# A streaming encoder on one core: rows turned in blocks for three pairs, and projections of whole width

## The chip, the cores and the metric

The kernel runs on one core of a Trainium2 chip. The metric is the device time of one execution in microseconds. Five engines work on it, each with an instruction stream of its own that runs in order: TensorE (PE; its weight loads are listed apart as PEld), VectorE (DVE), ScalarE (ACT), GpSimd (POOL) and SyncE (SP), which here only issues transfers. Transfers run on 16 DMA engines.

## The reference

One layer of a streaming encoder with 2048 new frames of one stream ("prompt") and 64 of a running one ("sample"), width 1024. Cut to what matters:

```python
aq, ak, av, ag, hq, hf, hi, hg = jnp.split(rms_norm(x, ln_g) @ w_in, SPLITS, axis=-1)
k, v = heads(ak), heads(av)                      # 8 heads of 64
o_a = attn_fn(heads(aq), k, v) * silu(ag)        # chunks of 64 frames, 576 keys, learned bias
o_b, S = hgrn2_branch(hq, hf, hi, hg, lb, norm_g, s0)   # 4 heads of 128, gated recurrence
y = x + concat([o_a, o_b]) @ w_out
...
y_prompt = rms_norm(hp, ln_f_g)
new_k_prompt, new_v_prompt                       # the last 512 frames' K and V rows
```

The outputs that the change touches are the last 512 rows of K and V, one row per frame, and the last rows of `y_prompt`.

## The kernel before

**Tiling.** The frames are taken in four super-blocks of 512, 576 (with the sample's 64), 512 and 512 frames (`SUPER`). In each, 32 projections follow (`JOBS`): for each of four groups hf, hq, hi, hg (one recurrence head) and pg, pq, pk, pv (gate, Q, K and V of a pair of attention heads). In the last super-block the last twelve come in another order, and end with pk and pg of the last pair. One projection gives 128 features by the frames of the block: `project` does 24 matmuls, since x and the weights are split into a high and a low part (w_hi x_hi, w_hi x_lo, w_lo x_hi, eight pieces each). Normally it runs over all 512 frames at once (128x512). The first two projections of a super-block run in halves of 256 frames, interleaved (first half of one, first half of the other, then the second halves), since the second half's x (tiles xh and xl) is filled later; the last two run in halves too, which lets the next block's x replace the first half early.

**Behind a projection** stands its evacuation, which takes the accumulator "acc" out of PSUM. Features lie on the partitions, so K and Q are used as they come. V must have frames on the partitions. There are two ways for that. `ev_v` (super-blocks 1 to 3) transposes 32x32 blocks on DVE straight from the accumulator into a tile "vT" (`turn_blocks`), moves the blocks into place through a scratch in DRAM (`turn_rows`: four transfers out, "way<-vT", and one back, "vT<-way"), and splits the result into high and low parts (`split_rows`: a cast on ACT, a subtraction on DVE). `ev_v_last` (last super-block) copies to "vT", transposes on PE (`tr<-ident,vT`), and splits from PSUM. The K and V rows of the last super-block go out by `new_rows`: four transposes on PE, a copy to a tile "sig", one transfer of 256 KB.

**Order.** The program is written out by a planner (`Plan`) before it is compiled: each stage is a Python thread that yields until its data, its engine's queue or a token is there; `project` emits two matmuls and lets the others go on. The planner's own times decide the order on each engine and are not run times. Tokens stand for buffers: "sig" two, "vT" three, "acc" two, weights "w" four, "ck" one. The gates (`silu_to`: three ACT steps into a "sig" tile and a DVE product into "sga") use "sig" too.

**The end.** When the last projection is done, `out_load` reads the mixed heads back ("sig<-mixd", "vT<-mixd"), and the output product follows: 56 steps of 12 matmuls of 128x512 with weights that come from scratch (`wo_load`, "w<-wod"), beside the last attention. `out_norm` ends each tile of 128 frames: a square on ACT for each half of 512 columns, 1/sqrt on ACT, the product with r and the gain on DVE, and a transfer.

Of the kernel before, what the change touches and what calls it, by code (L numbers as in the profile page):

```python
# [8 lines left out]
F32 = mybir.dt.float32  # L9
# [3 lines left out]
ALU = mybir.AluOpType  # L13
# [4 lines left out]
P = 128  # L18
D = 1024
# [4 lines left out]
NPAIR = 4  # L24
# [22 lines left out]
JOBS = [[(k, g) for g in range(4) for k in ("hf", "hq", "hi", "hg", "pg", "pq", "pk", "pv")] for _ in SUPER]  # L47
# [136 lines left out]
def hymba_step(  # L184
# [439 lines left out]
    def new_rows(src, off, bn, p, out_p, out_s, tok, t):  # L624

        full = bn // P
        segs = [(a, b, rows, out) for a, b, rows, out in ((0, full, P, out_p), (full, full + 1, bn - full * P, out_s))
                if rows and out is not None]
        if not segs:
            tok.put(1, t)  # L630
            return
        yield from tk["tr"].get()
        yield t
        pt = tr_ps()
        for a, b, rows, out in segs:
            for j in range(a, b):
                transpose(pt[:rows, j * P : (j + 1) * P], src[:, j * P : j * P + rows], ident)
        t = C.pe()
        tok.put(1, t)
        for a, b, rows, out in segs:  # L640
            s3 = pt[:rows, a * P : b * P].rearrange("p (t d) -> p t d", d=P)
            yield from tk["sig"].get()
            yield "D", t
            st = T(wk, [P, 512], F32, "sig", bufs=2).rearrange("p (t d) -> p t d", d=P)
            dve.tensor_copy(st[:rows, : b - a], s3)
            t = C.dve((b - a) * P)
            yield t
            row = off + a * P
            if rows == P:
                sp.dma_start(out[row : row + (b - a) * P, p * P : (p + 1) * P].rearrange("(t q) d -> q t d", q=P),  # L650
                             st[:, : b - a])
            else:
                sp.dma_start(out[:, p * P : (p + 1) * P], st[:rows, 0])
            tk["sig"].put()
        tk["tr"].put(1, t)

    def split_rows(src, v, h, t0, nt, rows, t):
        s = src.rearrange("p (h a t j) -> p h a t j", h=2, a=2, t=nt)[:, h]
# [80 lines left out]
    def pair_jobs(sb, p):  # L739
        t0, n = SUPER[sb][:2]  # L740
        last = sb == len(SUPER) - 1
        smp = n > WIN
        d = Pair()
        d.sb, d.p = sb, p
# [45 lines left out]
        def ev_k(acc, off, bn, t):  # L790
            yield from tk["vT"].get()
            yield "A", t
            kn = T(wk, [P, 512], F32, "vT", bufs=VTB)
            act.copy(kn[:, :bn], acc)
            t = C.act(bn, t)
            tk["acc"].put(1, t)
            c = slice(512 + off, 512 + off + bn)
            for h in range(2):
                yield lambda: d.open[h]
                yield "A", t  # L800
                act.copy(d.kd[own[h], h, c], kn[own[h], :bn])
# [6 lines left out]
            yield from new_rows(kn, off, bn, p, nk_prompt if last else None, nk_sample, tk["vT"], t)  # L808
            yield from got_all(True)

        def ev_v_last(acc, off, bn, t):
# [28 lines left out]
        def ev_v(acc, off, bn, t):  # L840
            yield from tk["vT"].get()
            yield "D", t
            vt = T(wk, [P, 512], F32, "vT", bufs=VTB)
            t = turn_blocks(vt, acc, bn)
            tk["acc"].put(1, t)
            t = yield from turn_rows(vt, bn, t)
            full = bn // P * P
            parts = [p_ for p_ in ((0, full, P, None),
                                   (full, P if bn > full else 0, bn - full, nv_sample)) if p_[1]]
            for c, w, rows, out in parts:  # L850
                if out is not None:
# [1009 lines left out]
    def out_norm(o, tile_, half, t):  # L1861
# [25 lines left out]
        if x[3] is not None and not end:  # L1887
            yield "D", t
            dve.scalar_tensor_tensor(x[3][:rows], x[3][:rows], r[:rows], g_in[:rows], ALU.mult, ALU.mult)
            t = C.dve(1070, t)  # L1890
            yield t
            sp.dma_start(y, x[3][:rows])
            C.dma(512 * rows / P)
        else:
            for a in range(2):
                c = slice(a * 512, a * 512 + 512)
                yield "D", t
                dve.scalar_tensor_tensor(x[a][:rows], x[a][:rows], r[:rows], g_in[:rows, c], ALU.mult, ALU.mult)
                t = C.dve(530, t)
                yield t  # L1900
                sp.dma_start(y[:, c], x[a][:rows])
                C.dma(256 * rows / P)
# [48 lines left out]
    def program():  # L1951
# [66 lines left out]
        for sb in range(nsb):  # L2018
# [6 lines left out]
            for u, (kind, g) in enumerate(JOBS[sb]):  # L2025
# [13 lines left out]
                    C.spawn((recurrence if kind[0] == "h" else attention)(d), 1)  # L2039
                evac = made[kind[0], g][1][kind[1]]  # L2040

                if u in (1, len(JOBS[sb]) - 1):
                    for half in range(2):
                        yield from project(j - 1, [halves[half]], before, half == 1,
                                           lambda part, k0: x_ready(sb, half, part, k0))
                        yield from project(j, [halves[half]], evac, half == 1,
                                           lambda part, k0: x_ready(sb, half, part, k0))
                        if u > 1:
                            x_left[sb, half] = True
                elif u not in (0, len(JOBS[sb]) - 2):  # L2050
                    yield from project(j, blocks, evac)
                before = evac
                j += 1
        for i, k in steps:
# [147 lines left out]
```

## Time and profile before

| | |
|---|---|
| median of 3 runs | 1247.86 us (1247.58 to 1248.82) |
| profiled execution | 1248.42 us, its span 1246.1 us |
| granted TensorE clock | 0.999 |
| DMA queue of SP | 144120 packets, 289.86 MB, 69.0% of 16 engines' span |
| longest wait of PE on another engine | 1.4 us, near the start |

In rows of the trace, the first number is the start in us, the second the length; then engine, line, operation, what is written and read, and the shape. A line such as "DMA out_dram<-sig" in the chain of waits is a transfer from its issue to its landing. PE's ends overlap, since matmuls are pipelined: the price of one is read from start to start.

### The profile page before, as it was taken

Reading aid. Unit: us, or ns where it says so; the run is one execution under the profiler, and the core shown is the slowest. Engines: PE = TensorE matmul, PEld = TensorE weight load, DVE = VectorE, ACT = ScalarE, POOL = GpSimd, SP = SyncE. Lnnn points to the kernel's source line nnn. Section 1 sums busy time; section 2 is a strip of 40 time slices with the busy share of each in tenths; the row PEclk is TensorE's granted clock in tenths of the full one; section 3 lists DMA queues with packets and bytes.
Section 4 is the critical chain, followed back from the end, with each engine's and each line's share of the span. In section 5 each row is a group of like instructions: output and inputs, shape, how many; then the busy total and the mean of one; then the engine's idle time right before and its main releaser. Section 6 shows DMA issues by size and latency. Waiting matters only on the chain. (4 is left out here: it accounts for less than half of the span.)

```text
span 1246.1 us, 21403 instructions
## 1 busy us (share of the span) xinstructions
PE 1234.7 (99%) x7494; PEld 1085.9 (87%) x7494; DVE 893.0 (72%) x1901; ACT 683.0 (55%) x1534; POOL 413.2 (33%) x702
## 2 busy tenths in 40 slices
PE   9999999999999999999999999999999999999997
PEld 7888888999999999998888888988888888888786
DVE  7697878867767677786577667776757476867775
ACT  6354545755665556574465556665556445643443
POOL 7665564111120111201233242143242103474543
PEclk9999999999999999999999999999999999999999
DMA  8897888667575575655777778677686665988431
GB/s 337 301 321 258 320 293 327 204 185 252 155 217 148 158 252 186 204 164 189 279 267 251 271 263 281 227 257 252 231 273 206 218 209 208 343 266 245 144 118 68
DMA packets 144516, 291.22 MB, mean 234 GB/s; under 512 B 38617, under 2 KB 85337, under 8 KB 126746
## 3 DMA queue, kind: packets, MB, share of 16 engines
q1 hardware_dynamic: 144120, 289.86, 69.0%
q8 instruction: 59, 0.97, 0.3%
q14 instruction: 47, 0.39, 0.1%
q10 hardware_dynamic: 290, 0.01, 0.0%
HBM read 196.95 MB, written 93.91 MB: 233 GB/s over the span
## 5 line engine op out<-in xcount | busy, mean ns | idle before, releaser
L249 PE MATMUL acc<-xh,w 128*128 128x512 f32 (+2 forms) x2752 | 566.0, 345 | 1.2 <-DVE gq L580 0.7
L249 PEld LDWEIGHTS acc<-xh,w 128*128 128x128 f32 x2752 | 438.4, 189 | 51.7 <-ACT xh L409 0.9
L249 PE MATMUL acc<-xl,w 128*128 128x512 f32 (+2 forms) x1376 | 293.8, 345 | 0.5 <-DVE xl L415 0.5
L249 PEld LDWEIGHTS acc<-xl,w 128*128 128x128 f32 x1376 | 221.0, 189 | 25.2 <-DVE xl L415 0.7
L939 ACT ACTIVATE pr<-pr,nm 128x640 f32<-128x640 f32 (+4 forms) x132 | 100.4, 761 | 56.3 <-DVE nm L922 55.9
L951 ACT CAST ph<-tr 128x512 fp32r<-128x512 f32 (+3 forms) x176 | 87.8, 506 | 74.8 <-PE pv L249 50.1
L922 DVE CUSTOM_DVE_ANT_0 pr<-s,bias 128x640 f32<-128x640 f32 (+4 forms) x128 | 94.3, 737 | 46.6 <-PE s L249 45.7
L473 POOL TENSOR_TENSOR w<-wraw,w 128x256 fp32r<-128x256 f32 x120 | 102.3, 882 | 54.9 <-DVE w L468 41.8
L954 DVE TENSOR_TENSOR ph<-tr,ph 128x512 fp32r<-128x512 f32 (+3 forms) x176 | 100.8, 588 | 25.0 <-ACT ph L951 24.3
L249 PE MATMUL pv<-ph,v 128*128 128x256 f32 (+2 forms) x344 | 97.1, 368 | 0.0
L510 POOL TENSOR_TENSOR xn<-wraw,xn 128x256 fp32r<-128x256 f32 x48 | 41.2, 859 | 145.0 <-ACT xn L507 145.0
L253 PE MATMUL tr<-ident,pr 128*128 128x128 f32 x580 | 88.3, 273 | 0.3 <-DVE ph L954 0.3
L1570 POOL TENSOR_TENSOR k<-ob 128x512 f32<-128x512 f32 (+2 forms) x20 | 18.0, 902 | 198.4 <-ACT ob L1561 157.3
L1095 POOL TENSOR_TENSOR mixa<-mixa,sga 128x256 f32<-128x256 f32 (+1 forms) x36 | 28.0, 779 | 167.1 <-DVE mixa L993 141.4
L993 DVE TENSOR_TENSOR mixa<-mixa,pv 64x256 f32<-64x256 f32 (+1 forms) x144 | 56.8, 394 | 35.7 <-ACT mixa L989 32.2
L943 DVE TENSOR_SCALAR pr<-pr,sm 128x640 f32<-128x640 f32 (+4 forms) x132 | 75.8, 574 | 4.7
L253 PEld LDWEIGHTS tr<-ident,pr 128*128 128x128 f32 x580 | 69.6, 140 | 9.9 <-PE acc L249 0.7
L575 ACT ACTIVATE sig<-acc 128x512 f32<-128x512 f32 (+2 forms) x64 | 32.0, 500 | 76.4 <-PE acc L249 73.7
L249 PEld LDWEIGHTS pv<-ph,v 128*128 128x128 f32 (+1 forms) x344 | 58.6, 189 | 7.4 <-issue 0.3
L989 ACT COPY mixa<-pv 64x256 f32<-64x256 f32 (+1 forms) x72 | 25.1, 349 | 64.3 <-PE pv L249 58.4
L249 PE MATMUL s<-kd,q 128*128 128x320 f32 (+2 forms) x232 | 55.6, 309 | 0.0
L249 PE MATMUL s<-kd,ql 128*128 128x320 f32 (+2 forms) x232 | 55.5, 309 | 0.0
(338 smaller groups left out, 2131.2 us busy)
## 6 DMA issues: line engine op xcount, KB each, us to landing
w<-wd SPq DMA_DIRECT2D x96, 1024.0 KB, 5.4
wd<-w SPq DMA_DIRECT2D x32, 1024.0 KB, 7.1
wraw<-in_w_in_dram SPq DMA_DIRECT2D x30, 512.0 KB, 5.0
wod<-xn SPq DMA_DIRECT2D x28, 512.0 KB, 5.0
xn<-in_x_prompt_dram SPq DMA_DIRECT2D x23, 512.0 KB, 4.7
bias<-biasd SPq DMA_DIRECT2D x24, 320.0 KB, 5.8
carry<-kd SPq DMA_DIRECT2D x12, 512.0 KB, 5.8
carry<-v SPq DMA_DIRECT2D x12, 512.0 KB, 6.2
```

The costliest lines, as they stand in the source:

```text
L249: pe.matmul(out, w, x, **kw)
L253: pe.transpose(out, x, idn)
L473: pool.tensor_sub(w[:, 1, k : k + 2], raw[:, k : k + 2], f32(w[:, 0, k : k + 2]))
L510: pool.tensor_sub(f32r(st[:, c.start + 512 : c.stop + 512]), src[:, c], st[:, c])
L575: act.activation(sig[:, :bn], acc, AF.Exp, scale=-1.0)
L922: dve.tensor_tensor_reduce(s[:, :nk].rearrange("p (a c) -> p a c", a=ns), sps[:, :ns, :kn], d.bias[:, h, bcol : bcol + nk].rearrange("p (a ...
L939: act.activation(s[:, :nk], s[:, :nk], AF.Exp, bias=nm[:, 0:1], scale=-1.0, accum_out=sm)
L943: dve.tensor_scalar(s[:, :nk], s[:, :nk], sm, None, ALU.mult)
L951: act.copy(ph[:krows, 0, :wid], pt[:krows, :wid])
L954: dve.tensor_sub(ph[:krows, 1, :wid], pt[:krows, :wid], f32(ph[:krows, 0, :wid]))
L993: dve.tensor_add(mix[hs, :qn], mix[hs, :qn], pv[hs, i, :qn])
L1095: pool.tensor_mul(mix[:, :n], mix[:, :n], d.sg[:, g0 : g0 + n])
```

## The change

1. In the last super-block, pairs 0 to 2 (`by_blocks`) take V by `ev_v` as the other super-blocks do, and their V rows go out of "vT" by a new function `rows_to`: four transfers of 64 KB, in pieces of 128 bytes. Their K rows no longer take `new_rows` but the new `block_rows`: block transpose on DVE into "sig", the same detour, then `rows_to`.
2. The last pair keeps `new_rows`, with the V rows staged in "ck" in place of "sig". The tokens of the staging tiles are given back some us later in the planner's time.
3. In super-blocks 3 and 4 the first projection alone runs in halves and the second over all 512 frames. In the last super-block the last two run over all 512 too.
4. The very last tile's norm: one half is multiplied by the gain on DVE ahead of r, then by r on ACT, which also issues its transfer; the other half stays with DVE and SP.

```diff
@@ new_rows
+            tag = "ck" if out is nv_prompt else "sig"
+            yield from tk[tag].get()
...
-            tk["sig"].put()
+            tk[tag].put(1, C.now + (6000.0 if rows == P else 0.0))
...
+    def rows_to(src, out, off, w, p):
+        s4 = src.rearrange("q (a t j) -> q t a j", a=4, j=32)
+        for i in range(w // P):
+            row = off + i * P
+            sp.dma_start(out[row : row + P, p * P : (p + 1) * P].rearrange("q (a j) -> q a j", a=4), s4[:, i])
+            C.dma(64)
+            yield C.now + 800.0
+
+    def block_rows(src, off, bn, p, out, tok, t):
+        yield from tk["sig"].get()
+        yield "D", t
+        st = T(wk, [P, 512], F32, "sig", bufs=2)
+        t = turn_blocks(st, src, bn)
+        tok.put(1, t)
+        t = yield from turn_rows(st, bn, t)
+        yield t
+        yield from rows_to(st[:, :bn], out, off, bn, p)
+        tk["sig"].put(1, C.now + 4000.0)
@@ pair_jobs
+        by_blocks = last and p < NPAIR - 1
...
+            if by_blocks:
+                yield from block_rows(kn, off, bn, p, nk_prompt, tk["vT"], t)
+            else:
+                yield from new_rows(kn, off, bn, p, nk_prompt if last else None, nk_sample, tk["vT"], t)
@@ ev_v
+                elif by_blocks:
+                    C.spawn(rows_to(vt[:, c : c + w], nv_prompt, off + c, w, p), 2)
...
-            tk["vT"].put(1, t)
+            tk["vT"].put(1, t + (4000.0 if by_blocks else 0.0))
...
-        return d, dict(g=ev_g, q=ev_q, k=ev_k, v=ev_v_last if last else ev_v)
+        return d, dict(g=ev_g, q=ev_q, k=ev_k, v=ev_v_last if last and not by_blocks else ev_v)
@@ out_norm
+            if end and tile_:
+                yield "D", 0.0
+                c = slice(half * 512, half * 512 + 512)
+                dve.tensor_mul(x[half], x[half], g_in[:, c])
+                C.dve(530)
+                o["scaled"] = half
...
+        elif end and tile_:
+            a = o["scaled"]
+            act.mul(x[a], x[a], r)
+            act.dma_start(y[:, a * 512 : a * 512 + 512], x[a])
+            c = slice((1 - a) * 512, (1 - a) * 512 + 512)
+            dve.scalar_tensor_tensor(x[1 - a], x[1 - a], r, g_in[:, c], ALU.mult, ALU.mult)
+            sp.dma_start(y[:, c], x[1 - a])
@@ main
-                if u in (1, len(JOBS[sb]) - 1):
+                lone = sb > 1 and u == 0
+                if lone:
+                    for half in range(2):
+                        yield from project(j, [halves[half]], evac, half == 1,
+                                           lambda part, k0: x_ready(sb, half, part, k0))
...
+                elif u == 1 and sb < 2 or u == len(JOBS[sb]) - 1 and not last:
...
-                elif u not in (0, len(JOBS[sb]) - 2):
+                elif u != 0 and (last or u != len(JOBS[sb]) - 2):
                     yield from project(j, blocks, evac)
```

**PE at the start of super-block 3.** Here w_6650 are the weights of its first projection, w_6782 those of its second; acc is the accumulator, a suffix numbers the buffer. Before, the first projection's second half (acc_7194) comes behind the other one's first half (acc_7119):

```order
L249 MATMUL acc_7119<-xl_154,w_6782 128x256 x4
L249 MATMUL acc_7119<-xh_153,w_6782 128x256 x8
L249 MATMUL acc_7194<-xh_153,w_6650 128x256 x8
L249 MATMUL acc_7194<-xl_154,w_6650 128x256 x8
L253 MATMUL tr_7220<-ident_69,pr_6935 128x128
```

Now acc_7119 is the first projection's own second half, and the other follows whole:

```order
L249 MATMUL acc_7119<-xl_154,w_6650 128x256 x6
L249 MATMUL acc_7119<-xh_153,w_6650 128x256 x8
L249 MATMUL acc_7195<-xh_153,w_6782 128x512 x8
L249 MATMUL pv_7136<-ph_7155,v_570 128x512 x2
L253 MATMUL tr_7219<-ident_69,pr_6935 128x128
```

The second half of the first projection moved ahead by 24 matmuls, and the second projection has one pass of 24 in place of two.

**PE at V of pair 0 in the last super-block.** vT_10625 is K of the pair, vT_10708 V, acc_10705 the projection after V. Before, between the projections stand the transposes:

```order
L253 MATMUL tr_10693<-ident_69,vT_10625 128x128 x4
L249 MATMUL acc_10622<-xh_153,w_10411 128x512 x2
L249 MATMUL acc_10705<-xh_153,w_10475 128x512 x2
L249 MATMUL g_10710<-q_2036_10654,ones_74 128x512
L249 MATMUL g_10710<-q_2037_10655,ones_74 128x512
L249 MATMUL s_10717<-kd_569,q_571 128x320 x2
L249 MATMUL s_10717<-kd_569,ql_155 128x320 x2
L253 MATMUL tr_10723<-ident_69,vT_10708 128x64 x4
```

Now, from the last matmuls of V (acc_10564) on:

```order
L249 MATMUL acc_10564<-xh_153,w_10353 128x512 x4
L249 MATMUL s_10639<-kd_569,q_571 128x320 x2
L249 MATMUL s_10639<-kd_569,ql_155 128x320 x2
L249 MATMUL acc_10645<-xh_153,w_10417 128x512 x8
L249 MATMUL acc_10645<-xl_154,w_10417 128x512 x8
L249 MATMUL acc_10645<-xh_153,w_10417 128x512 x2
```

The transposes from vT are gone; the first product with pair 0's V of this super-block (pv_10839) comes 56 wide matmuls later. On SP, the same pair's rows now take these places (sig_10627 are K's rows, vT_10653 V's, w_10723 a later projection's weights):

```order
L711 DMA way_10648<-sig_10627 32x4x128 x4
L446 DMA w_10656<-wd_61_133 128x2048
L711 DMA way_10662<-vT_10653 32x4x128 x4
L512 DMA wod_70_142<-xn_9951 256x1x512
L1623 DMA mixd_15_87<-ob_10588 128x512
L715 DMA sig_10627<-way_10648 128x512
L446 DMA w_10723<-wd_45_117 128x2048
L715 DMA vT_10653<-way_10662 128x512
L662 DMA out_dram<-vT_10653 128x4x32
```

**SP at the end of the last super-block.** Before, V rows (sig_12747) and the first half of the K rows (sig_12761) go out ahead of the two output weight loads (w_12789, w_12830):

```order
L650 DMA out_dram<-sig_12747 128x4x128
L650 DMA out_dram<-sig_12761 128x2x128
L2108 DMA gin_152<-in_ln_f_g_dram 128x1024
L2062 DMA w_12789<-wod_66_138 128x2048
L2062 DMA w_12830<-wod_66_138 128x2048
L650 DMA out_dram<-sig_12868 128x2x128
L1680 DMA sig_12886<-mixd_12_84 128x4x128
```

Now the V rows (ck_12657) stand ahead of the weights (w_12595, w_12684) and the K rows (sig_12668) behind:

```order
L651 DMA out_dram<-ck_12657 128x4x128
L1706 DMA sig_12678<-mixd_12_84 128x4x128
L2156 DMA gin_152<-in_ln_f_g_dram 128x1024
L2110 DMA w_12595<-wod_66_138 128x2048
L2110 DMA w_12684<-wod_66_138 128x2048
L651 DMA out_dram<-sig_12668 128x4x128
L1706 DMA sig_12791<-mixd_12_84 128x4x128
```

**ACT at the same place.** acc_12590 is the last projection, sig_12755 its gate, pr_12730 a block of scores, ph the high part of turned scores; sig_12755 lies where sig_12668 lay:

```order
L977 CAST ph_12751<-tr_12740 128x512
L575 ACTIVATE sig_12755<-acc_12590 128x512
L576 ACTIVATE sig_12755<-sig_12755,one_77 128x512
L577 ACTIVATE sig_12755<-sig_12755 128x512
L965 ACTIVATE pr_12730,sm_12767<-pr_12730,nm_12731 128x640
L977 CAST ph_12785<-tr_12769 128x256
```

The gate is one of 512 columns, where there were two of 256, and the exponential of pr_12730 stands behind it.

More of the change, by code (lines that the diff above doesn't have):

```diff
@@ L641, in new_rows @@
             s3 = pt[:rows, a * P : b * P].rearrange("p (t d) -> p t d", d=P)
-            yield from tk["sig"].get()
+            tag = "ck" if out is nv_prompt else "sig"
+            yield from tk[tag].get()
             yield "D", t
-            st = T(wk, [P, 512], F32, "sig", bufs=2).rearrange("p (t d) -> p t d", d=P)
+            st = T(wk, [P, 512], F32, tag, bufs=1 if tag == "ck" else 2).rearrange("p (t d) -> p t d", d=P)
             dve.tensor_copy(st[:rows, : b - a], s3)
@@ L807, in ev_k @@
                 d.k_t[h] = max(d.k_t[h], t)
-            yield from new_rows(kn, off, bn, p, nk_prompt if last else None, nk_sample, tk["vT"], t)
+            if by_blocks:
+                yield from block_rows(kn, off, bn, p, nk_prompt, tk["vT"], t)
+            else:
+                yield from new_rows(kn, off, bn, p, nk_prompt if last else None, nk_sample, tk["vT"], t)
             yield from got_all(True)
@@ L2040, in program @@
                 evac = made[kind[0], g][1][kind[1]]
-                if u in (1, len(JOBS[sb]) - 1):
+                lone = sb > 1 and u == 0
[3 more added lines that the diff above has]
+                                           lambda part, k0: x_ready(sb, half, part, k0))
+                        if u:
+                            x_left[sb, half] = True
+                elif u == 1 and sb < 2 or u == len(JOBS[sb]) - 1 and not last:
                     for half in range(2):
@@ L2049, in program @@
                             x_left[sb, half] = True
-                elif u not in (0, len(JOBS[sb]) - 2):
+                elif u != 0 and (last or u != len(JOBS[sb]) - 2):
                     yield from project(j, blocks, evac)
+                    if u == len(JOBS[sb]) - 1:
+                        x_left[sb, 0] = x_left[sb, 1] = True
                 before = evac
```

## The prediction

> **What bounds the kernel now.** I read the page first, then the busy time by stage, then the waits of PE.
>
> ```profile
> PE 1234.7 (99%) x7494; PEld 1085.9 (87%) x7494; DVE 893.0 (72%) x1901; ACT 683.0 (55%) x1534; POOL 413.2 (33%) x702
> ```
>
> ```profile
> 540.00:600.00 60.00, 60.00 (x388) 53.27 (x387) 41.73 (x102) 32.18 (x73) 6.82 (x17) 1.00 0.52 169
> 850.00:950.00 100.00, 100.00 (x555) 84.71 (x554) 68.81 (x139) 58.09 (x122) 32.40 (x47) 1.00 0.72 242
> 950.00:1063.00 113.00, 113.00 (x683) 97.53 (x682) 71.53 (x148) 56.82 (x114) 22.48 (x45) 1.00 0.63 217
> 1063.00:1085.00 22.00, 21.70 (x120) 18.21 (x119) 17.21 (x40) 13.27 (x30) 11.11 (x14) 1.00 0.92 345
> ```
>
> Each stage row has its length, then the busy time of PE, PEld, DVE, ACT and POOL, the granted TensorE clock, the DMA share and GB/s. Super-block 3 begins near 540; the last one's attention projections lie in 850 to 1063; the output stage follows. PE is busy without a gap, at clock 1.00, in all the places that the change touches before 1063. So PE time removed there is time removed from the run, as long as nothing new makes PE wait. The reader is to see two more things: DVE and ACT have about a third free, and just after 1063 the DMA engines are 92% busy. That is where spare time is short.
>
> **Part 1: whole projections.** In super-blocks 3 and 4 the second projection, and in the last one the last two, become one pass of 24 matmuls of 512 columns instead of 48 of 256: 4 x 48 = 192 narrow ones go and 96 wide ones come. What each form costs in the stream:
>
> ```profile
> 21.81 2.08 PE L249 MATMUL acc<-xh,w 128*128 128x256 f32 x16
> 23.73 1.12 PE L249 MATMUL acc<-xl,w 128*128 128x256 f32 x8
> 24.69 2.96 PE L249 MATMUL acc<-xh,w 128*128 128x256 f32 x16
> 27.49 1.98 PE L249 MATMUL acc<-xl,w 128*128 128x512 f32 x8
> 29.30 3.79 PE L249 MATMUL acc<-xh,w 128*128 128x512 f32 x16
> 32.93 0.39 PE L249 MATMUL acc<-xl,w 128*128 128x512 f32 x1
> ```
>
> From start to start, 16 narrow ones take 23.73 - 21.81 = 1.92 us, 120 ns each; 16 wide ones take 32.93 - 29.30 = 3.63 us, 227 ns each. Two narrow ones cost 240, so each pair merged saves 13 ns, and 96 pairs save **1.25 us**.
>
> [...]
>
> **Part 2: K and V of pairs 0 to 2 in the last super-block.** PE loses, per pair, a group of four transposes for the K rows, one for the V rows, and two half-width groups for V itself: 24 of 128x128 and 24 of 64x64 in all.
>
> ```profile
> 863.70 0.60 PE L253 MATMUL tr<-ident,vT 128*128 128x128 f32 x4
> 864.06 1.18 PE L249 MATMUL acc<-xh,w 128*128 128x512 f32 x4
> ...
> 865.84 0.46 PE L249 MATMUL s<-kd,ql 128*128 128x320 f32 x2
> 866.22 0.46 PE L253 MATMUL tr<-ident,vT 64*128 64x64 f32 x4
> 866.62 1.65 PE L249 MATMUL acc<-xh,w 128*128 128x512 f32 x6
> ```
>
> A group of four takes 0.36 us (863.70 to 864.06), a half-width one 0.40, plus about 0.08 by which the two scores matmuls ahead of it are stretched (865.84 to 866.22 is 0.38 for two that otherwise take 0.29, as in 1063.02 to 1063.32 below). Per pair 2 x 0.36 + 2 x 0.48 = 1.68, for three pairs **5.0 us**. All of it stands in the stretch where PE never idles.
>
> What replaces it is off PE. On DVE, six block transposes and six splits come for six copies and six splits that go; with 69 of 100 us busy there it has room. On SP come 24 transfers to the scratch and 6 back, and 24 stores in place of 6. What the detour takes is to be read from super-blocks 1 to 3, which send V that way already:
>
> ```profile
> way<-vT SPq DMA_DIRECT2D x72, 64.0 KB, 4.9
> vT<-way SPq DMA_DIRECT2D x18, 256.0 KB, 5.5
> ```
>
> ```profile
> 607.24 0.72 DVE L671 STREAM_TRANSPOSE vT<-acc 128x512 f32<-128x512 f32 x1
> ...
> 627.45 0.42 DVE L663 TENSOR_TENSOR v<-vT,v 128x256 fp32r<-128x256 f32 x1
> ```
>
> By medians the detour is 0.72 (transpose) + 1.3 (three issues ahead of the last, 0.43 each, as the row of that line shows further down) + 4.9 + 0.3 + 5.5 + 0.5 + 0.4 = 13.6 us; by this one instance in super-block 3 it is 20.2. In the new order, in the last super-block, the first matmul that reads pair 0's new V comes after about 16.8 us of PE work from the end of V's projection (56 wide matmuls, 20 of scores and 14 transposes between them, at the prices above); for pair 1 it is about 20.5, for pair 2 over 24. So pair 0 waits 0 to 3.4 us; I take 0.5, near the medians. K itself does not take the detour, only its rows that go out, and nothing waits for those but their buffer.
>
> In super-block 3 and 4 the first projection's second half now comes directly behind its first half. Its input is the last x tile:
>
> ```profile
> 543.25 0.59 ACT L409 CAST xh<-g 128x512 fp32r<-128x512 f32 x1 [1.78 <-PE g L253]
> ```
>
> The first matmuls that need it would come near 544.1, and this cast ends at 543.84. It just fits; I take 0.1 a boundary, 0 to 0.5 each. Waits of pair 0 and of the boundaries: **+0.7**.
>
> **Part 3: the last pair's rows and what stands behind them.** V rows go to "ck" and K rows to "sig", both free of each other. But the order now puts the K rows' transfer on SP behind the two 1 MB weight loads, and the last gate (three ACT steps into "sig") gets the same place in memory as the K rows. Behind the gate ACT has the exponential of a block of scores, in order. Before, the same chain had a shorter form; this is the trace's chain of waits and the transfers' landings:
>
> ```profile
> 1059.40 6.07 DMA out_dram<-sig
> ...
> 1065.56 0.39 ACT sig L575
> ...
> 1066.93 0.82 ACT pr L939 x2
> 1067.75 4.70 DMA out_dram<-sig
> ...
> 1079.32 0.73 DVE pr L943
> ```
>
> ```profile
> L2062 SPq DMA_DIRECT2D w<-wod x2: 320/426/532, 1061.1 to 1063.2; - x2
> ...
> DMA to landing us min/median/max: 8.4/8.7/8.9
> ```
>
> ```profile
> 1063.02 0.46 PE L249 MATMUL s<-kd,q 128*128 128x320 f32 x2
> 1063.32 0.46 PE L249 MATMUL s<-kd,ql 128*128 128x320 f32 x2
> ```
>
> Call T the end of the last projection (1063.02 before: there the scores' matmuls above follow it). The second weight load started at T + 0.2 and landed 8.9 later, at T + 9.1; a row transfer issued at 1067.75 landed 4.70 later, 0.35 behind those weights. So transfers behind weights end with them. In the new order the K rows are issued at about T + 0.6 and land near T + 9.5. Then: three gate steps of 512 columns, 1.8 (before 1.37 for 256 columns; a 512-wide ACT step takes about 0.6), to T + 11.3; the exponential 0.9 to T + 12.2; DVE's division 0.75 and two hand-overs 0.1 to T + 13.05. PE reaches the transposes of that block after 34 wide matmuls (7.72), 16 of scores (2.32) and 10 transposes (0.97), at T + 11.0. PE waits **2.0 us**. Bounds: alone in the queue the K rows would land as below, with no wait; with the longest landing of that line's loads, 14.0, they would end at T + 14.6 and the wait would be 7.1. I take the value from the nearest row. The 4 MB of output weights are queued behind the gate too, and are about as late as PE then is.
>
> ```profile
> out_dram<-sga SPq DMA_DIRECT2D x2, 256.0 KB, 2.0
> ```
>
> ```profile
> DMA to landing us min/median/max: 8.0/9.4/14.0
> ```
>
> The first row is from the page's list of transfers (KB each, median us to landing), the second from the line that loads the output weights.
>
> **Part 4: the last norm.**
>
> ```profile
> 1239.66 0.69 DVE L1821 TENSOR_TENSOR pr<-pr,acc 128x512 f32<-128x512 f32 x1 [2.05 <-issue]
> 1240.27 1.41 DVE L1898 SCALAR_TENSOR_TENSOR bias<-bias,rstd,gin 128x512 f32<-128x512 f32 x2
> ...
> 1241.70 1.42 DVE L1898 SCALAR_TENSOR_TENSOR pr<-pr,rstd,gin 128x512 f32<-128x512 f32 x2
> 1242.52 0.96 SPq L1901 DMA_DIRECT2D out_dram<-pr  x2
> ```
>
> One half of the last tile moves to ACT, but the order on DVE puts one of the other tile's two products behind: it then ends at 1241.70 + 2 x 0.71 = 1243.1 as the last product does now, and its store is the third on SP. Nothing is won: **+0.2** (-0.3 to +1.0).
>
> **The sum**, on the profiled execution (1248.42 us; the span of 1246.1 lies in it): -1.25 - 5.0 + 0.7 + 2.0 + 0.2 = -3.35, so 1245.07. The profiled execution is 0.56 above the median of the three runs, 1247.86, so against that it is **1244.5 us**.
>
> **Rivals.** *B, the K rows do not wait for the weights* (0.25). If transfers overtake, the wait of 2.0 goes and little of the 0.7 is left: -6.25 + 0.2 + 0.2 = -5.85, 1242.0. For it: stores of 256 KB land in 2.0 when the queue is quiet. Against it: the 4.70 and the 0.35 above.
>
> [...]
>
> *C, the gain is mostly eaten* (0.20): K rows at the upper part of their bounds (4 us of wait) and V of pair 0 like the instance of 20.2 (3.4 less what overlaps, 1 to 2): -6.25 + 0.2 + 4 + 1.5 = -0.55, 1247.3.
>
> *D, slower: the detour through SP* (0.11). All the added transfers (24 and 6 for the detours, 18 more stores) pass the one SP queue, which runs in order and holds weight loads that wait for a free slot; a load that waits between the trips out and back holds V back. With the longest landings of these lines, below, a detour is 0.72 + 1.3 + 11.3 + 0.3 + 8.3 + 0.9 = 22.8; two more us of waiting at the head of the queue make it 24.8, which costs pair 0 8.0 and pair 1 4.3: -6.25 + 0.2 + 2.2 + 12.3 = +8.4, about 1256. It decides once these waits together exceed some 6 us. Against it: in super-block 3 nothing waited on PE for V.
>
> ```profile
>   ACT v L660: 10.4, 5
> ...
> DMA to landing us min/median/max: 1.9/3.1/8.3
> ```
>
> ```profile
> L691 SPq DMA_DIRECT2D way<-vT x184: 302/431/1844, 32.8 to 1009.3; - x184
> ...
> DMA to landing us min/median/max: 1.4/4.1/11.3
> ```
>
> The first answer is for the line of the trips back, the second for that of the trips out; of waits of PE for either there is none.
>
> That the transposes would come back elsewhere on PE is not possible: the order has them no more, and PE's rows fall from 2659 to 2641.
>
> **The numbers.** Forecast A has 0.44 around 1244.5 (1243.3 to 1246), B 0.25, C 0.20, D 0.11. About 0.2% (2.5 us) is what a measurement of this kernel can tell from no change: faster is below 1245.4, slower above 1250.4. All of B and some three quarters of A are faster, 0.58; the rest of A and C are the same, 0.31; D is slower, 0.11. The range 1241.5 to 1249.0 takes in B, A and C, and leaves out most of D.
>
> **What would show it.** PE busy time down by about 6.2 us; no transposes from vT at 850 to 1060 but the last pair's; PE idle about 2 us some 11 us behind the last projection, released by DVE, with ACT waiting for "out_dram<-sig" ahead of the gate; pair 0's first product with V late by under 1 us. I am wrong if the K rows land before T + 7.5 (then B), if ACT waits for "vT<-way" for longer than 3 us with PE idle behind it (D), or if the 13 ns a pair are not there.

## The result

The changed kernel takes 1254.54 us (median of 5 runs, 1254.33 to 1259.01), the kernel before 1248.82 in the runs beside it (1247.58 to 1249.87): a ratio of 1.0057, 95% interval 1.0046 to 1.0068. It is slower by 5.7 us, where 1244.5 was forecast. The profiled execution of the changed kernel took 1254.5. Two executions in a slow state (2027.93 us in experiment 8, and 3137.38 of the kernel before beside experiments 9 to 11) enter no ratio below.

Its span is 1252.7. The first part of its page (busy time, share of the span, instructions):

```profile
PE 1231.0 (98%) x7350; PEld 1075.7 (86%) x7350; DVE 898.1 (72%) x1895; ACT 678.9 (54%) x1520; POOL 410.5 (33%) x702
```

PE has 144 matmuls less and is busy 3.7 us less (about 6.2 was the sign to look for; part of the difference is the half clock shown below: four matmuls of 128x512 took 0.46 us each from start to start at 1075.94 to 1077.79, where four took 0.26 each at clock 1.00, at 1070.96 to 1071.98), and still the span is 6.6 us longer. So PE stands still where it did not. Its last projection shows how far the saving went. In the timeline of PE, this row follows it directly (start, length, then the instruction):

```profile
1058.41 0.45 PE L249 MATMUL s<-kd,q 128*128 128x320 f32 x2
```

Before, the same place was at 1063.02. That is 4.6 us earlier, after one new wait of 2.1 us which the next view shows; so about 6.7 us of PE work are gone ahead of this place. About 0.4 of that has only moved behind it (four matmuls of scores went behind, 0.58 us; two transposes came ahead, 0.18), which leaves 6.3, and 6.25 were forecast. From here to the end 11.2 us are lost. The waits of PE between 1000 and 1126, in the changed kernel (engine, line, whom it waited for: us in total, times, longest; pr is a block of scores, nm its extreme value, tr its transposes, ph the high part of the turned scores, w<-wod a load of output weights, xh the high part of an operand of the output product):

```profile
PE tr L253 <- DVE pr L969: 3.1, 1, 3.1
PE pv L249 <- DVE ph L980: 2.1, 1, 2.1
PE acc L249 <- DMA w<-wod: 1.6, 1, 1.6
PE s L249 <- DVE nm L948: 0.7, 2, 0.5
PE pv L249 <- ACT xh L1751: 0.5, 1, 0.5
```

The same view of the kernel before, 1000 to 1125, has two waits of 0.3 us:

```profile
PE tr L253 <- DVE ph L954: 0.3, 1, 0.3
PE acc L249 <- DVE slot L1733: 0.3, 1, 0.3
```

**The largest, 3.1 us.** The chain of waits of the changed kernel, around the last gate (start, length, what):

```profile
1061.44 10.17 DMA out_dram<-sig
...
1071.72 0.61 ACT sig L575
...
1073.64 0.92 ACT pr L965 x2
...
1074.78 0.56 DVE pr L969
...
1075.38 0.90 PE tr L253 x3
```

The K rows of the last pair go out at 1061.44 and land 10.17 us later. Only then does the gate start, behind it the exponential, the division and PE, which goes on 17.0 us after the last projection where 13.05 was forecast. It is the path that the prediction described, but longer. SP shows why (same columns as the timeline of PE):

```profile
1058.86 0.39 SPq L651 DMA_DIRECT2D out_dram<-ck  x1
...
1060.50 0.85 SPq L2110 DMA_DIRECT2D w<-wod  x2
1061.44 0.85 SPq L651 DMA_DIRECT2D out_dram<-sig  x1
```

The V rows stand at the head of SP's queue and wait 3.6 us for their copy on DVE, which ends at 1058.84. So the two weight loads go out 2.1 and 2.6 us after the last projection, where they went 1.9 us ahead of it and 0.2 after it before. PE waits 1.6 us for them too.

**After the wait, the clock.** The stages of 2 us around it (length, busy PE, PEld, DVE, ACT, POOL, granted clock, DMA share, GB/s):

```profile
1072.00:1074.00 2.00, 0.25 (x2) 0.00 (x0) 0.17 (x1) 1.94 (x4) 0.00 (x0) 1.00 0.00 0
1074.00:1076.00 2.00, 0.62 (x4) 0.62 (x4) 1.91 (x5) 0.84 (x4) 0.00 (x0) 0.73 0.03 10
1076.00:1078.00 2.00, 2.00 (x7) 1.61 (x6) 1.75 (x5) 1.97 (x5) 0.00 (x0) 0.50 0.99 286
1078.00:1080.00 2.00, 2.00 (x15) 1.87 (x15) 1.14 (x4) 0.87 (x3) 0.00 (x0) 0.92 1.01 318
```

From about the time when PE goes on, it is granted half its clock. Missing clock: 2 x (0.27 + 0.50 + 0.08) = 1.7 us' worth. In the execution before, no 2 us stage from 200 us to the end of PE's work is below 1.00.

**The wait of 2.1 us, at 1022.** The chain there:

```profile
1007.17 7.89 DMA w<-wd
...
1015.08 3.09 DMA way<-vT
...
1018.31 4.36 DMA vT<-way
...
1022.69 0.63 ACT gi L1305
...
1023.34 0.59 ACT ph L977
...
1024.70 0.74 PE pv L249 x2
```

This "vT" is not V of a pair: it is released to "gi", the input of a recurrence head (hi of head 3). It has the same detour, and in the changed order the K rows of pair 2 have theirs on SP directly ahead of it, behind a weight load. ACT waits for the input in order, and the cast that makes the high part of the turned scores (ph) stands behind it. Before, ACT had two such casts directly ahead of "gi", and nothing waited there.

**The tail.** The last matmul before and after, and the landings of the last four stores (us, min/median/max), before in 1240 to 1247 and after in 1244 to 1253:

```profile
1239.18 0.39 PE L249 MATMUL acc<-v,slot 128*128 128x512 f32 x1
```

```profile
1244.39 0.39 PE L249 MATMUL acc<-v,slot 128*128 128x512 f32 x1
```

```profile
DMA to landing us min/median/max: 2.0/2.0/2.1
```

```profile
DMA to landing us min/median/max: 2.7/3.0/3.1
```

From there to the end of the span it was 6.9 us (1246.1 - 1239.2) and is 8.3 (1252.7 - 1244.4): 1.4 more.

### The profile page after: what moved, and what is told of

Read it like the earlier page. It is cut to its first block, busy times and chain, and to the rows that moved or that the text cites. A ratio compares the mean times of both kernels' runs of the same rounds, so it can differ in the third digit from the quotient of the medians.

```text
span 1252.7 us, 21135 instructions
## 1 busy us (share of the span) xinstructions
PE 1231.0 (98%) x7350; PEld 1075.7 (86%) x7350; DVE 898.1 (72%) x1895; ACT 678.9 (54%) x1520; POOL 410.5 (33%) x702
## 4 chain that ended last, share of the span: by engine, by line
PE 81%; DMA 8%; DVE 4%; POOL 2%; issue 2%; ACT 1%; SPq 1%; DVEq 0%; POOLq 0%; ACTq 0%
PE acc L249 57%; PE g L249 7%; PE tr L253 6%; PE pv L249 5%; PE s L249 5%; DMA w<-wd 2%; DMA wraw<-mixd 1%; DMA vT<-way 1%; DMA way<-vT 1%; DMA out_dram<-xn 1%; DMA b11l<-wod 1%; DMA out_dram<-sig 1%; POOL xn L1852 1%; POOL sig L1777 1%; PE g L253 1%
## 5 line engine op out<-in xcount | busy, mean ns | idle before, releaser
L249 PEld LDWEIGHTS acc<-xh,w 128*128 128x128 f32 x2688 | 431.7, 189 | 52.2 <-ACT xh L409 0.9
```

The lines of the kernel that those rows point to most:

```text
L249: pe.matmul(out, w, x, **kw)
```

## The experiments

Each was timed beside the kernel before, in four sets (1 to 4, 5 to 8, 9 to 11, 12); ratios are to it, with 95% intervals. Its medians in the four sets: 1248.99, 1249.19, 1249.18 and 1248.65 us. Only one execution of each version was profiled; where single runs spread, its time is given. "Changed kernel" and "kernel before" say which of the two an experiment starts from.

### 1. The staging tiles swapped

```diff
-            tag = "ck" if out is nv_prompt else "sig"
+            tag = "ck" if out is nk_prompt else "sig"
```

> The changed kernel with the two staging tiles of the last pair swapped: V rows in sig, K rows in ck; order on all engines as in the changed kernel. Theory 1 (the last gate waits for the K rows' landing, because it takes their place in memory, and ACT, DVE and PE stand behind it): the gate starts within 3 us of the last projection's end (1058.4 in the changed kernel's profile, its gate at 1071.7), PE's wait of 3.1 us on DVE pr goes, the granted clock stays at 1.00 between 1070 and 1080, and the time falls by 3.3 (the wait) + 1.7 (the slow clock) + about 1 (the two waits behind it), to about 1248.5. Rival (the transfers around it are late in any case, the wait on w<-wod for one): PE waits 3 us at the same place, about 1254.

Measured: 1251.24 us, 1.0013 (1.0001 to 1.0025), 3.3 below the changed kernel; single runs from 1248.36 to 1254.63. The gate in its timeline on ACT:

```profile
1068.62 0.60 ACT L575 ACTIVATE sig<-acc 128x512 f32<-128x512 f32 x1
```

It waits for no transfer any more (no idle time is shown ahead of it); it comes in its place behind ACT's other work (6.5 us after the last projection, so the expected "within 3 us" was wrong). PE's wait of 3.1 us on pr is gone, and the clock there is 1.00. PE still waits for the weights (1.1) and for a ph (1.5). And the profiled execution lost its clock elsewhere, behind the wait at 1024, which was 2.3 here:

```profile
1028.00:1030.00 2.00, 2.00 (x9) 1.70 (x8) 1.39 (x2) 1.20 (x3) 0.00 (x0) 0.53 0.86 344
1030.00:1032.00 2.00, 2.00 (x11) 1.84 (x10) 0.13 (x2) 1.42 (x3) 0.00 (x0) 0.62 0.27 111
```

Theory 1 holds for the gate. Of the ten runs four lie at 1248.4 to 1248.8, the time that it gave, and six at 1250.9 to 1254.6; the profiled one (1251.96) is of the second kind. PE's wait for the weights, 1.1 us, has another cause than the gate.

### 2. The old norm

```diff
-            if end and tile_:
...
-        elif end and tile_:
...
```

> The changed kernel with the last norm as before. Theory 1 (three transfers on SP and one on ACT come within a microsecond and land later, 3.1 instead of 2.1 us, and the last is issued 0.3 later): from the last matmul to the end 6.9 us as before instead of 8.3, time about 1253.1. Rival (the tail's difference is the run's, not the norm's): 8.3 stays, 1254.5.

Measured: 1254.17 us, 1.0049 (1.0032 to 1.0066). The last matmul starts at 1244.94 in the profiled execution and the span is 1251.9: 7.0 us of tail instead of 8.3. The four stores are issued over 2.1 us again and land in 2.0 to 2.1. So the trace agrees with theory 1; whether the stores land later because they come close together or because one goes out from ACT was not parted. The median moved by only 0.4, less than the four runs of this version differ (1253.66 to 1257.36).

### 3. V of pairs 0 to 2 alone

From the kernel before, V of the change's part 2 (with `rows_to`):

```diff
+        by_blocks = last and p < NPAIR - 1
...
+                elif by_blocks:
+                    C.spawn(rows_to(vt[:, c : c + w], nv_prompt, off + c, w, p), 2)
...
-        return d, dict(g=ev_g, q=ev_q, k=ev_k, v=ev_v_last if last else ev_v)
+        return d, dict(g=ev_g, q=ev_q, k=ev_k, v=ev_v_last if last and not by_blocks else ev_v)
```

> The kernel before with V of pairs 0 to 2 of the last super-block by blocks on DVE and the detour, nothing else of the change: K rows by PE as before, projections in halves, old norm. Theory 1 (the wait of 2.1 us at 1022 comes from the K rows of pair 2, whose detour stands ahead of the recurrence input's on SP): no PE wait over 1 us between 860 and 1040; saved 3 x (0.96 + 0.36) = 4.0 us, so about 1244.8 where before is 1248.8. Rival (V's own detour makes PE wait): waits of 1 to 3 us at one or more of the pairs, 1246 to 1249.

Measured: 1250.16 us, 1.0012 (1.0002 to 1.0021). Half of theory 1 held: PE has no wait between 860 and 1040, so V's own detour costs nothing there. The time did not follow: after 1040 the waits are new ones, 4.8 us in all where before has 0.6. The three longest:

```profile
PE tr L253 <- DVE v L856: 1.4, 1, 1.4
PE tr L253 <- DVE ph L980: 1.2, 1, 1.2
PE s L249 <- DVE nm L948: 1.1, 1, 1.1
```

By the prices 4.0 us were saved, and not even the time of before was reached. What PE saved ahead of the end of the last super-block it lost there by waiting.

### 4. The second projection of super-blocks 3 and 4 alone, whole

```diff
-                if u in (1, len(JOBS[sb]) - 1):
+                lone = sb > 1 and u == 0
...
+                elif u == 1 and sb < 2 or u == len(JOBS[sb]) - 1:
```

> The kernel before with the second projection of super-blocks 3 and 4 whole, nothing else. By the price of 13 ns a merged pair, 48 pairs save 0.62 us: about 1248.2 where before is 1248.8, if the second half's x is there in time; if it is not, waits of up to 0.5 us at 544 and at the next boundary eat it (1248.8 or more).

Measured: 1248.77 us, 0.9997 (0.9988 to 1.0006). No difference is seen; 0.6 us is within the interval, and so is nothing. It is inconclusive for the price of 13 ns, and shows no harm from the half that follows directly.

### 5. K rows of pair 2 by PE again

From the changed kernel:

```diff
-            if by_blocks:
+            if by_blocks and p < NPAIR - 2:
```

> The changed kernel, but with the K rows of pair 2 alone taken out by PE again. Theory 1 (the wait of 2.1 us at 1022 is the recurrence's input, whose detour stands on SP behind the K rows' detour): that wait goes, PE pays 0.36 us for the four transposes, about 1252.6 where the changed kernel is 1254.5. Rival (weights queued on SP ahead of both set that landing): PE still waits over 1.5 us for pv near 1022, 1254.5.

Measured: 1253.93 us, 1.0045 (1.0028 to 1.0061), single runs 1251.00 to 1259.39. The wait at 1022 fell to 0.5; this is the whole list of PE's waits from 1000 to 1040:

```profile
PE pv L249 <- DVE ph L980: 0.5, 1, 0.5
```

The K rows' detour made most of that wait, but not all of it. With it, PE waited 2.1, 2.3, 1.7 and 3.1 us here (changed kernel, experiments 1, 2 and 9); without it 0.5, 1.0 and 0.9 (experiments 5, 6 and 12). In this run the input landed only 0.6 us earlier, and PE came to the place 1.0 later (0.36 of transposes, and a wait of 0.7 at 887). The other part is ACT's order. Here ACT still waits 3.2 us for the input; in experiment 8, which keeps the K rows' detour, it waits longer, but the casts of 512 columns that PE needs do not stand directly behind, and PE does not wait. ACT's row there, in experiments 5 and 8 (in brackets how long ACT stood idle, and for what):

```profile
1022.07 0.62 ACT L1305 COPY gi<-vT 128x512 f32<-128x512 f32 x1 [3.16 <-DMA vT<-way]
```

```profile
1019.64 0.62 ACT L1305 COPY gi<-vT 128x512 f32<-128x512 f32 x1 [4.14 <-DMA vT<-way]
```

The time fell by 0.6, not 1.9, and the interval does not tell that from nothing: the gate and the weights at the end remain, and PE waited 3.0 us there for nm.

### 6. All three suspects out

Experiment 5, the old norm, and the swap for the last pair only:

```diff
-            tag = "ck" if out is nv_prompt else "sig"
+            tag = "ck" if out is nk_prompt and p == NPAIR - 1 else "sig"
```

> The changed kernel with the three suspects out together: staging tiles of the last pair swapped, K rows of pair 2 by PE, old norm. Theory 1: the three prices add up: 1254.5 - about 5 (gate, its wait and the slow clock) - 1.9 (wait at 1022 less 0.36) - 1.4 (tail) = about 1246, faster than before (1249.0). Rival (the stage 1050 to 1100 is bound by transfers, so PE time saved ahead of it is given back there whatever the order): the waits between 1050 and 1100 come to 3 us or more, 1248.5 or above.

Measured: 1247.88 us, 0.9989 (0.9978 to 1.0000), single runs 1245.61 to 1250.63. That is 6.7 us below the changed kernel, so the three suspects together hold the whole loss, but not the 8.5 of the sum. The time lies between the two theories: five runs are at 1245.6 to 1246.9, where theory 1 has it, and five at 1248.9 to 1250.6. The profiled one (1249.38) is of the slower five. In it the waits between 1050 and 1100 came to 3.3 us, as the rival had it; the main one has a place that can be named:

```profile
PE acc L249 <- DMA w<-wod: 2.5, 2, 2.3
```

### 7. V by blocks, all four projections whole, K rows by PE

From the changed kernel, with the swap for the last pair and the old norm:

```diff
-            if by_blocks:
+            if False:
                 yield from block_rows(kn, off, bn, p, nk_prompt, tk["vT"], t)
```

> The kernel before with V of pairs 0 to 2 by blocks, the four projections whole and the last pair's K rows staged in ck; K rows of all pairs by PE, old norm. In this order the last gate stands ahead of the row copies and the two weight loads ahead of the rows. Saved on PE: 4.0 + 1.25 = 5.2 us. Theory 1: no gate behind a landing, so few waits, about 1244.5. Rival (the end is bound by transfers): about 1248.5 as all versions with less PE work.

Measured: 1246.10 us, 0.9978 (0.9968 to 0.9987), single runs 1244.55 to 1249.01: **faster than both kernels**. In this order SP has the weights ahead of the rows, and no gate stands behind a landing. Its profiled execution is one of its longest runs (1249.01), and shows one wait of 2.2 us, which ends at 1078.94, and the clock behind it:

```profile
1078.00:1080.00 2.00, 1.06 (x6) 1.01 (x7) 2.00 (x4) 0.15 (x1) 2.00 (x3) 0.94 1.01 426
1080.00:1082.00 2.00, 2.00 (x8) 1.70 (x8) 1.18 (x4) 0.71 (x2) 0.60 (x1) 0.50 0.97 406
1082.00:1084.00 2.00, 2.00 (x10) 1.71 (x9) 0.60 (x2) 1.46 (x4) 0.00 (x0) 0.70 0.33 127
```

### 8. K rows and V by blocks alone

From the kernel before, part 2 of the change only (`by_blocks` with `block_rows`, `rows_to` and `ev_v` as in the diff above).

> The kernel before with part 2 of the change only: K rows and V of pairs 0 to 2 by blocks; projections in halves, rows of the last pair in sig, old norm. Theory 1: PE saves 5.0, waits 2.3 near 1022 and no 3 us at the last gate (its K rows go out in halves, ahead of the weights): about 1246.5. Rival (any version that reaches the end earlier waits there for transfers): waits of 3 us or more between 1050 and 1100, 1249 or above.

Measured: 1247.45 us, 0.9985 (0.9975 to 0.9994): faster by 1.7 us, not 2.7. PE has no wait at 1022 here: on SP the input's detour stands ahead of the K rows', and ACT's order differs, as shown in experiment 5. So the K rows' detour does no harm in this order; against experiment 3, which lacks it, this version is even 2.7 us lower. But at 1054 there is a wait of 2.3 us for ACT's copy and behind it one of 0.9 for DVE, and the half clock lasts longer than anywhere else:

```profile
1056.00:1058.00 2.00, 0.80 (x2) 0.50 (x2) 1.94 (x4) 1.18 (x3) 2.00 (x3) 0.50 0.73 275
1058.00:1060.00 2.00, 1.64 (x8) 1.64 (x9) 1.97 (x5) 0.00 (x0) 0.43 (x1) 0.50 0.00 1
1060.00:1062.00 2.00, 2.00 (x11) 2.00 (x11) 1.21 (x3) 0.00 (x0) 0.00 (x0) 0.50 0.32 96
1062.00:1064.00 2.00, 2.00 (x15) 2.00 (x14) 0.46 (x1) 1.21 (x2) 0.20 (x1) 0.80 1.01 285
```

### 9. PE kept busy in the wait

From the changed kernel; the order is otherwise the same:

```diff
         pt = tr_ps()
+        for _ in range(fill):
+            pe.matmul(pt[:, :P], ident, ident, start=True, stop=True)
...
+                            11 if d.sb == 3 and d.p == NPAIR - 1 and h == 0 and g0 == 256 and i == 0 else 0), 1)
```

> The changed kernel with 11 matmuls of the identity by itself (about 0.25 us each, 2.75 us of PE work whose result is overwritten) put ahead of the transposes for which PE waits 3.1 us at 1072; nothing else. Theory (the granted clock falls to 0.50 there because PE stood idle): the clock stays at 1.00 between 1074 and 1080, the row of that stage shows 1.00 instead of 0.73, 0.50 and 0.92, and the time falls by about 1.7 us to 1252.8, though PE does more. Rival (the clock falls for another reason, or the fall costs nothing): 1254.5 or up to 2.7 more.

Measured: 1255.79 us, 1.0055 (1.0037 to 1.0073). The eleven matmuls took 2.45 us from start to start (1073.20 to 1075.65), 0.22 each. The clock did as the theory said:

```profile
1074.00:1076.00 2.00, 1.92 (x18) 1.68 (x16) 0.83 (x2) 1.97 (x5) 0.00 (x0) 1.00 0.00 0
1076.00:1078.00 2.00, 1.33 (x7) 0.96 (x7) 1.97 (x6) 0.84 (x4) 0.00 (x0) 1.00 0.41 124
1078.00:1080.00 2.00, 2.00 (x16) 1.87 (x15) 1.85 (x6) 1.95 (x5) 0.00 (x0) 1.00 0.88 259
```

This fits the theory that PE's idling halves the clock. It is one execution, and the wait of 3.1 us at 1022 in the same execution left the clock at 1.00, so that chance is not excluded. The time did not fall; it lies where the rival has it. In the profiled execution the stretch from the pv at the gate to the next product with output weights b11h is 1.5 us shorter (1068.26 to 1083.17 in the changed kernel, 1070.03 to 1083.42 here), but the wait at 1022 was 3.1 us in place of 2.1, in the same order. For the total time these four runs settle nothing.

### 10. All four projections whole, nothing by blocks

From the kernel before, with the swap of experiment 6.

> The kernel before with the four projections whole and the last pair's K rows staged in ck (V rows in sig); all rows and V by PE as before, old norm. By the price of 13 ns a merged pair 1.25 us are saved: 1247.9 where before is 1249.2. Rival (weights and carried rows at the end, queued together, make PE wait whenever it comes there earlier): 1249 or above, with a wait of over 1 us between 1055 and 1085.

Measured: 1252.99 us, 1.0032 (1.0019 to 1.0044): slower by 3.8, the rival's sign and more. Beside experiment 4 this puts the loss on the last two projections together with the swap and its later tokens, which this edit brings too; the two were not parted. It is no price of whole projections as such: experiment 7 has them with the same swap, and is the fastest version. SP has the weights behind the V rows again. PE waits 5.5 us between 1040 and 1126, where before has 0.6, and the main waits are:

```profile
PE acc L249 <- DMA w<-wod: 1.9, 2, 1.7
PE acc L249 <- DVE xn L1847: 1.3, 1, 1.3
PE acc L249 <- DMA v<-wod: 1.3, 1, 1.3
```

### 11. V by blocks, the last two projections in halves

From the kernel before: experiments 3 and 4 together, V rows of the last pair in "ck".

> The kernel before with V of pairs 0 to 2 by blocks, the second projection of super-blocks 3 and 4 whole, the last two projections in halves, the last pair's V rows staged in ck; K rows by PE, old norm. Saved on PE: 4.0 + 0.6 = 4.6. Theory 1 without a gate behind a landing: about 1245. Rival (the end gives back what is saved ahead of it): 3 to 5 us of waits between 1050 and 1125, 1247 to 1249.

Measured: 1247.61 us, 0.9986 (0.9977 to 0.9996): faster by 1.6 where 4.6 were saved on PE. PE has waits of 1.4, 1.4, 0.7 and 0.3 us between 1040 and 1126. This lies at the rival's time.

### 12. The weights ahead of the rows

Experiment 6, and in `new_rows`:

```diff
-            yield t
+            yield t + (3000.0 if rows == P and p == NPAIR - 1 else 0.0)
             row = off + a * P
```

> The version with the three suspects out (staging tiles swapped, K rows of pair 2 by PE, old norm), and the last pair's row transfers given out 3 us later in the planner's time, which puts the two 1 MB weight loads ahead of them on SP and the gate ahead on ACT. Theory 1 (PE's wait of 2.3 us on w<-wod, and the half clock behind it, come from the weight loads' place on SP: they are issued 1.5 and 2.0 us behind the last projection's end, 2.0 ahead of it and 0.1 behind before the change): the loads are issued before the projection ends, the wait on w<-wod goes and the clock stays at 1.00, 1247.9 - 2.3 to 4 = 1244 to 1245.6. Rival (another wait takes its place, since the transfers bound the stage): 2 us or more of waits on other releasers at 1060 to 1080, 1247 to 1248.

Measured: 1247.45 us, 0.9993 (0.9984 to 1.0002), single runs 1246.47 to 1249.96, the profiled one 1248.35. The order came out as meant; the weights are issued ahead of the rows:

```profile
1055.48 3.86 SPq L2097 DMA_DIRECT2D w<-wod  x2
1059.44 0.39 SPq L651 DMA_DIRECT2D out_dram<-sig  x1
```

The wait on w<-wod and the half clock are gone. In their place, later in the same stage:

```profile
PE acc L249 <- DVE xn L1847: 1.4, 1, 1.4
PE acc L249 <- DMA v<-wod: 1.2, 1, 1.2
```

Theory 1 was right on the wait and the clock, the rival on the time; its waits came, but at 1107 to 1116, not at 1060 to 1080.

## Why the prediction was wrong

**Part 1, whole projections (-1.25).** The matmuls went as forecast; the price of 13 ns could not be told from nothing in time (experiment 4). What failed is that the edit was counted as PE work only. Making the last two whole moves what stands behind them: with rows and V as before, and with the swap, the time rose by 3.8 us (experiment 10), while with V by blocks the same projections are in the fastest version (experiment 7).

**Part 2, the transposes (-5.0).** Right in size: with part 1, the last projection ended 4.6 us earlier after a wait of 2.1, of which 0.4 is order, so 6.3 in place of 6.25. V's detour was right too: pair 0 did not wait, in the changed kernel and in experiment 3. Wrong was the sentence that nothing waits for the K rows but their buffer. Their detour stands on SP ahead of a recurrence input's, ACT waits for that one ahead of a cast that PE needs, and PE lost 2.1 us at 1022, where +0.5 was put down for pair 0. About 1.5 of such a wait goes with the K rows' detour (2.3 on average in four runs with it, 0.8 in three without, experiment 5); the rest goes with ACT's order. The +0.2 for the boundaries cannot be told in these runs. Two slips in this part's and the next one's arithmetic change nothing: the instance of 20.2 us ends at the start of the last split (20.6 with it), and ten transposes at the price given are 0.90, not 0.97.

**Part 3, the gate (+2.0).** This is the term that failed most. The mechanism was right (experiment 1), the size was off: 1.6 + 3.1 us of waits at the gate, two of 0.5 behind it, and 1.7 for the clock, 7.4 together. Three things were missed. The K rows were taken to be issued at T + 0.6, a figure without a row behind it; they went at T + 3.0 (1061.44 against 1058.41), because the V rows ahead of them wait for DVE, and the weights with them, and they took 10.2 us instead of 8.9. The weights' lateness was put at nothing ("about as late as PE then is"); PE waited 1.6 us for them. And a wait of PE was priced at its length, although here the clock was halved afterwards (0.50 at 1076 to 1078).

**Part 4, the norm (+0.2).** It was 1.4, above the bound of 1.0. The order of the products came as worked out; but the four stores, issued within a microsecond, land in 2.7 to 3.1 us instead of 2.0 to 2.1.

**The sum.** 7.4 in place of 2.0, 2.1 in place of 0.5 and 1.4 in place of 0.2 are 8.2 us more than forecast. The forecast was 3.35 below the profiled execution before; with these it is 4.9 above, and it was 6.1 above. The remaining 1.2 us were not taken apart; one more new wait, of 1.2 us, ends at 1126.0.

**The rivals.** B fell: PE's wait for the weights ended at 1070.96, and the rows landed at 1071.61, behind them. D had the sign and nearly the time (1256; it was given 0.11), but by luck: its cause, V made late by the detour, did not happen. C named the gate rightly, at 4 us of wait, and V of pair 0 wrongly. What none of them said is the common trait of the experiments: each version that saves 4 to 6 us on PE gave back 3 us or more between 1040 and 1126 in its profiled execution, by whichever wait its order made the latest (DVE's v, the weights w<-wod, the gate, v<-wod, ACT's copy). Before, PE waits 0.6 us there in all. Taking one wait away showed the next (experiments 6 and 12). That it is one common bound, such as the DMA time (92% at 1063 to 1085 in the kernel before, 75% in the changed one), was not tried and stays open. Against a hard bound speak the five fastest runs of experiment 7, at 1244.6 to 1245.8: they keep 3.4 to 4.6 of the 5.2 us saved.

## What to carry to other kernels

Here, where PE was busy for 99% of the time, what was taken from it did not reach the end: 6.3 us were gone ahead of the last projection, and 11.2 were lost behind it, in a stage that depends on transfers issued at PE's pace. So look for slack in such a stage first, and for what each queue holds ahead. For every transfer that is added or moved, name the one directly behind it on the queue, whoever owns it, and what stands behind that one on the engine that waits for it. And put a price on the clock behind a wait of TensorE, beside its length: seven of the nine waits of over 2 us in these traces were followed by about half the clock, with 1.7 us of clock missing in six cases and 3.4 in one.

## What the runs showed of the hardware

**Behind seven waits clock was lost, in pieces of one size.** Behind these waits, of 2.2 to 3.2 us, the granted clock fell to 0.50 to 0.56 in a stage of 2 us, and the missing clock has one size: 1.7 us in the changed kernel, 1.7 in experiment 1 (2 x (0.47 + 0.38)), 1.7 in experiment 7 (2 x (0.06 + 0.50 + 0.30)), 1.7 in experiments 2, 5 and 6 as well, and twice that, 3.4, in experiment 8 (2 x (0.50 + 0.50 + 0.50 + 0.20)). At half clock that is 1.7 / 0.5 = 3.4 us of time, and twice that in experiment 8. It begins near the end of the wait, not at a fixed distance: in experiment 1 PE goes on at 1026.82 and the clock falls after 1028, in experiment 8 it falls at 1056.0 and PE goes on at 1056.63. And it does not follow each time: a wait of 2.1 us at 1022 in the changed kernel and one of 3.1 in experiment 9 left it at 1.00; why these two did was not shown. Behind waits of 1.7 us and less (experiments 2, 3 and 10 to 12) no fall is seen.

In the single runs of experiment 7 the slower ones have the lower clock. Of the ten, the five at 1244.6 to 1245.8 us have a mean granted clock of 0.999, and the four above 1247.4 have 0.997 or 0.998. The clock is not the whole of it: in experiment 6 two of the five slower runs have 0.999 as well. How far the median of so few runs moves without any change in the order was not measured; effects of 1 to 2 us, as in experiments 2, 5 and 9, are therefore read from the trace and not from the time.
